# Even mixer of a two-layer trunk: q and k projected first, the convolution's block products inside the attention, the input norm's root on VectorE, the last product by column halves

## The chip, the cores and the metric

The kernel runs on one core of a Trainium2 chip. Its time is the device time of one execution in microseconds (us), and what is compared is the median over runs.

## The reference

A decoder trunk of two layers over 256 tokens of 1024 channels, all in fp32. Each layer is a SwiGLU network (2752 wide), a token mixer and a second SwiGLU network, each on the RMS norm of its input. The mixer of the first layer, the even mixer, is what the change touches:

```
proj = h @ w_in                      # 1024 -> 512 value, 512 gate, 512 q, 128 k, 128 v
u = a_val * sigmoid(a_gate)
u = causal depthwise convolution of u (31 taps, 512 channels) + bias
u = silu(layer_norm(u))
q, k = rms_norm(q), rms_norm(k)      # per head of 64; 8 q heads, 2 kv heads
o = sliding-window attention (window 128, a learned sink per head)
x = x + concat([u, o]) @ w_out
```

## The kernel before

Every weight is fp32 and is multiplied as two parts: `unit` loads half a column block (4 x 128 rows by up to 512 columns) into a `raw` tile, ScalarE rounds it into `hi`, and VectorE writes `lo` = raw - hi. Three raw tiles, four hi and four lo tiles go round. `plan` lists the units in the order of use, `take` hands out the next one and prepares those up to four (`WB`) ahead. A product of 128 tokens with a unit is 12 matmuls: hi with both halves of the input, then lo. The input comes from `Norm`: VectorE applies the gain (`xg`), ScalarE writes the high part of `xt` and VectorE the low part; the square sums go to `rstd_of`, on GpSimd, and the root of the norm (`nr`) is multiplied in after the product.

The even mixer (`even_rest`) has TensorE and VectorE in an order written out by hand; ScalarE's order is a scheduler's. The convolution is shared out: 256 channels run on VectorE, tap after tap (62 steps on tiles `acc`, handed out by `run(taps, n)`), and 256 as 64 block products on TensorE (`pc`, handed out by `run(conv, n)`), each two matmul instructions in the trace. TensorE's share needs its tokens sorted by parity (`PARITY`), and the root of the norm in that order (`parities`, tile `rp`).

Before the change the steps are: projection of value and gate for VectorE's share; of value and gate for TensorE's share (tokens by parity); of q; of k and v; then 20 block products; the norms of q and k; their transposes (`pq`, `pk`); 8 block products; the attention's eight heads, each with scores (`sc`), the softmax's maximum on VectorE and its exponential on ScalarE (`p`), three transposes two heads later (`pp`) and the values (`o`) three heads later, with block products and three taps in between (`fill`); the transposes of the convolution's result (`cn`), its layer norm, transposes back (`yt`), a silu; and the output product in two halves of its inputs, first the attention's half (`mixer_first`, tile `oth`), then the convolution's (`mixer_last`, tile `uth`), each over four banks `m` (two token tiles by two column halves `d`). Then x is updated (`x`), transposed (`pt`) and goes into the next network's first products (`pj`).

Of the kernel before, what the change touches and what calls it, by code (L numbers as in the profile page):

```python
# [16 lines left out]
F32 = mybir.dt.float32  # L17
# [11 lines left out]
S = 256  # L29
# [12 lines left out]
def tile_trunk(ctx: ExitStack, tc: tile.TileContext, x, norm_g, w_gate, w_up, w_down,  # L42
# [18 lines left out]
    def sbank(name):  # L61
        return psum.tile([128, 512], F32, name=name, tag="sc", bufs=2)
# [74 lines left out]

    EV_CUTS = (((512, 256), (0, 256)), ((768, 256), (256, 256)), ((1024, 512),), ((1536, 256),))
    OD_CUTS = (((0, 512),), ((512, 512),), ((1024, 512),), ((1536, 512),))
# [15 lines left out]
    def prepare(n):  # L155
        while len(ready) < min(n, len(plan)):
            run(unit())
# [32 lines left out]

    def take():
        prepare(cursor[0] + WB)
        cursor[0] += 1
        return ready[cursor[0] - 1]
# [84 lines left out]
    class Norm:  # L279
# [15 lines left out]
        def parities(self):  # L295

            ps = tbank("rT")
            for t in range(2):
                nc.tensor.transpose(ps[:, t * 128:t * 128 + 128], self.r[t].to_broadcast([128, 128]), ident)
            rp, junk = sm("rp", 2), nat("junk")  # L300
            for r in range(2):
                nc.vector.tensor_tensor(junk[:, 0:128], ps[:, r:S:2], ident, op=ALU.mult)
                nc.vector.tensor_reduce(rp[:, r:r + 1], junk[:, 0:128], axis=AX.X, op=ALU.add)
            return rp
# [3 lines left out]

    def projects(xp, cols, tokens=HALVES):

        ps = [bank(f"pj{t}") for t in range(2)]

        def steps():
            for kh in range(2):
                hi, lo = take()
                for t in range(2):
                    h, l = (xp.xt[kh][:, i, :, tokens[t]] for i in range(2))
                    yield from products(ps[t], h, l, hi, lo, cols, FULL, kh == 0, kh == 1)
        return ps, steps()
# [72 lines left out]
    def after_(nxt, t, d):  # L392
        if nxt is None:
            nc.sync.dma_start(out=out[0, t * 128:(t + 1) * 128, d * 512:(d + 1) * 512], in_=xs[t][d])
        else:
            nxt.part(t, d)
            if t == 1 and d == 1:
                nxt.finish()

# [72 lines left out]

    def attention_out(os_, ls, fill=lambda t: None):
        rl = work.tile([128, 8, 2], F32, name="rl", tag="rl", bufs=1)
        nc.vector.reciprocal(rl, ls)
        on = []
        for t in range(2):
            on.append(nat("on"))
            nc.vector.tensor_tensor(on[t].rearrange("p (h e) -> p h e", e=64),
                                    os_[t].rearrange("p (h e) -> p h e", e=64),  # L480
                                    rl[:, :, t:t + 1].to_broadcast([128, 8, 64]), op=ALU.mult)
        pts = [transposed(on[t]) for t in range(2)]
        res = []
        for t in range(2):
            fill(t)
            res.append(split_tile(pts[t], "ot"))
        return res
# [3 lines left out]

    def mixer_first(ys, src):

        for d in range(2):
            hi, lo = take()
            for t in range(2):
                yield from products(ys[t][d], *src[t], hi, lo, 512, FULL, True, False)

    def mixer_last(ys, src, nxt):


        units = [take() for d in range(2)]
        n = 4 // len(src[0])
        todo = []
        for j in range(len(src[0])):
            last = j == len(src[0]) - 1
            for d in range(2):
                hi, lo = units[d]
                for t in range(2):
                    h, l = src[t][j]  # L510
                    ks = slice(n * j, n * j + n)
                    product(ys[t][d], h, l, hi[:, ks], lo[:, ks], 512, FULL[:n], False, last)
                    if last:
                        run(todo, len(todo) - 1)
                        nc.vector.tensor_tensor(xs[t][d], ys[t][d], xs[t][d], op=ALU.add)
                        todo.append(partial(after, nxt, t, d))
        return todo
# [17 lines left out]
    def even_rest(xp, nxt, gv):  # L535
# [25 lines left out]
        def pe_conv():  # L561
            pc = sbank("pc")
            for g in range(4):
                for q in range(16):
                    w = wT[4 * g + q // 4][:, 2 * (q % 4):2 * (q % 4) + 2].rearrange("p i c -> p (i c)")
                    yield partial(nc.tensor.matmul, pc[:, g * 128:(g + 1) * 128], w,
                                  vT[g // 2][:, g % 2, q + 1:q + 129], start=q == 0, stop=q == 15)
            for g in range(4):
                yield partial(nc.scalar.activation, cv[:, g], pc[:, g * 128:(g + 1) * 128], AF.Identity,
                              bias=bias2[:, g:g + 1])  # L570

        cv = work.tile([128, 4, 128], F32, name="cv", tag="cv", bufs=1)
        taps = [partial(dve_tap, c, k) for k in range(TAPS) for c in range(2)]
# [8 lines left out]

        rp = xp.parities()
        u = [nat("u") for t in range(2)]
        for t in range(2):
            gated(gv[t], xp.r[t], u[t][:, :256].rearrange("p (g c) -> p g c", c=64))
        gv, steps = projects(xp, 512, PARITY)
        for t in range(2):
# [4 lines left out]
        run(steps, 6)  # L593
        run(taps, 6)
        run(steps)
        run(taps, 8)
        u2 = nat("u2").rearrange("p (g r c) -> p g r c", g=4, r=2)
        for t in range(2):
            gated(gv[t], rp[:, t:t + 1], u2[:, :, t])
        qps, steps = projects(xp, 512)  # L600
        run(steps, 12)
        pt = transposed(u2.rearrange("p g r c -> p (g r c)"))
        for j in range(2):
            nc.scalar.activation(vT[j][:, :, PADB:PADB + 128], pt[:, 2 * j:2 * j + 2], AF.Copy)
        run(steps, 12)
        run(taps, 7)
        run(steps)
        run(taps, 6)
        hs = work.tile([128, 20], F32, name="hs", tag="hs", bufs=1)
        qns = [head_sums(qps[t], xp.r[t], 8, hs[:, 8 * t:8 * t + 8], "q") for t in range(2)]  # L610
        run(taps, 4)
        kps = project(xp, 256)
        run(taps, 3)
        kns = [head_sums(kps[t], xp.r[t], 2, hs[:, 16 + 2 * t:18 + 2 * t], "k") for t in range(2)]
        rh = inv_sqrt(hs, 1.0 / 64, 20)
        run(conv, 20)
        vn = []
        kT = work.tile([128, 512], F32, name="kT0", tag="kT0", bufs=1)
        qT = [slot("qT", "l") for t in range(2)]
        kns = [head_norm(kns[t], rh[:, 16 + 2 * t:18 + 2 * t], 2) for t in range(2)]  # L620
        qns = [head_norm(qns[t], rh[:, 8 * t:8 * t + 8], 8, paired=True) for t in range(2)]
        for t in range(2):
            k_to_T(kns[t], vo[:, 17:18], 1, [kT], t)
        for t in range(2):
            q_to_T(qns[t], gq_e, qT[t])
        for t in range(2):
            v = work.tile([128, 512], F32, name="vn", tag="vn", bufs=2)
            nc.scalar.activation(v[:, :128], kps[t][:, 128:256], AF.Copy, scale=xp.r[t])
            vn.append(v)
        run(conv, 8)  # L630
        run(taps, 4)

        def fill(i):
            run(taps, 3)
            run(conv, 6 if i < 3 else 3)

# [11 lines left out]
        nc.vector.tensor_tensor(ls, ls, es, op=ALU.add)  # L648
        run(taps)
        run(conv)  # L650

        cps = [sbank("cn") for j in range(2)]
# [6 lines left out]
        of = [[cps[0][:, r * 256:(r + 1) * 256], cps[1][:, (1 - r) * 256:(2 - r) * 256]] for r in range(2)]  # L659
        o = attention_out(os_, ls)  # L660
        st, mv = sm("st", 24), sm("mv", 4)
# [4 lines left out]
        r_ = inv_sqrt(mv.rearrange("p (t m) -> p t m", m=2)[:, :, 1], 1.0, 2)  # L666
        ys = mixer_banks()
        steps = mixer_first(ys, o)
        run(steps, 20)
        yn = [nat("yn") for r in range(2)]  # L670
        for j in range(2):
            for r in range(2):
                nc.vector.tensor_scalar(yn[r][:, j * 256:(j + 1) * 256], of[r][j], mv[:, 2 * r:2 * r + 1], r_[:, r:r + 1],
                                        op0=ALU.subtract, op1=ALU.mult)
        us = [[], []]
        for j in range(2):
            run(steps, 6)
            ps = tbank("yt")
# [13 lines left out]
            for t in range(2):  # L692
                us[t].append([w[:, :, HALVES[t]] for w in (hi, lo)])
        run(steps)
        return mixer_last(ys, us, nxt)
# [171 lines left out]
```

## Time and profile before

| | |
|---|---|
| median of three runs | 959.21 us (958.87 to 959.63) |
| the profiled execution's own time | 959.92 us |
| its span in the trace | 957.9 us, 11336 instructions |
| busy share: TensorE matmul, weight load, VectorE, ScalarE, GpSimd | 98%, 81%, 56%, 47%, 10% |
| the even mixer, from its first product to the point from which the next network runs on | 196.67 to 311.56 us |

The time outside the span is 2.0 us. Windows count in us from the span's start. PE is TensorE's matmuls, PEld its weight loads, DVE VectorE, ACT ScalarE, POOL GpSimd. A matmul's end in the trace is modelled, so that two that follow each other overlap in their records; how fast TensorE goes is read from one start to the next.

### The profile page before, as it was taken

The numbers are of one execution on the slowest core, as the hardware profiler recorded it, in microseconds if no ns is written. First come the engines' busy times: TensorE is split into PE (matmuls) and PEld (weight loads), VectorE is DVE, ScalarE is ACT, GpSimd is POOL, SyncE is SP. The second block draws the span as 40 slices with busy tenths as digits, with TensorE's granted clock in tenths as the row PEclk, the third lists the DMA queues.
The fourth block names the chain that finished last, engine by engine and source line by source line (L and its number), as shares of the span: only waits on it lengthen the run. The fifth ranks groups of instructions, "written<-read, shape, count | busy, mean of one in ns | idle before, by whom it ended". The sixth has DMA issues, their size and how long they took to land.

```text
span 957.9 us, 11336 instructions
## 1 busy us (share of the span) xinstructions
PE 936.5 (98%) x4431; PEld 775.5 (81%) x4431; DVE 537.0 (56%) x735; ACT 451.4 (47%) x654; POOL 100.6 (10%) x158
## 2 busy tenths in 40 slices
PE   7999999989898999999999999999999999999998
PEld 5888887868886888888778888887788888888876
DVE  6855464668766655545546554635562275555551
ACT  6644454345444544444445444534567464444430
POOL 3000000740000200000002000000153260000000
PEclk9999999999999999999999999999999999999999
DMA  8865555646204465555665555556653066555540
GB/s 291 274 210 176 176 176 181 194 132 176 89 1 158 150 220 176 155 190 182 197 203 193 176 176 172 180 184 222 213 182 132 3 223 216 184 186 179 187 143 23
DMA packets 91974, 164.75 MB, mean 172 GB/s; under 512 B 3824, under 2 KB 17968, under 8 KB 91920
## 3 DMA queue, kind: packets, MB, share of 16 engines
q1 hardware_dynamic: 91120, 163.07, 52.3%
q0 software_dynamic: 736, 0.93, 0.3%
q8 instruction: 35, 0.57, 0.2%
q14 instruction: 19, 0.16, 0.0%
q10 hardware_dynamic: 64, 0.02, 0.0%
HBM read 162.96 MB, written 1.05 MB: 171 GB/s over the span
## 4 chain that ended last, share of the span: by engine, by line
PE 95%; DVE 3%; ACT 1%; DMA 1%; issue 0%; POOL 0%; DVEq 0%; POOLq 0%
PE pj L333 57%; PE y L199 25%; PE pt L236 3%; PE m L199 2%; PE m L333 2%; DVE lo L330 1%; PE pc L333 1%; PE sc L437 1%; DMA sink_b<-in_ev_sinks_dram 1%; PE pp L451 1%; ACT hi L330 0%; PE sc L438 0%; PE o L459 0%; PE o L458 0%; PE o L457 0%
## 5 line engine op out<-in xcount | busy, mean ns | idle before, releaser
L330 DVE TENSOR_TENSOR lo<-raw,hi 128x1024 fp32r<-128x1024 f32 (+2 forms) x306 | 358.5, 1207 | 237.6 <-ACT hi L330 231.4
L330 ACT ACTIVATE hi<-raw 128x1024 fp32r<-128x1024 f32 (+3 forms) x311 | 308.5, 1039 | 319.3 <-PE pj L333 145.7
L333 PE MATMUL pj<-hi,xt 128*128 128x512 f32 (+2 forms) x1664 | 411.5, 387 | 2.6 <-ACT xt L330 1.9
L333 PEld LDWEIGHTS pj<-hi,xt 128*128 128x128 f32 x1664 | 309.1, 189 | 63.0 <-ACT xt L330 2.6
L333 PE MATMUL pj<-lo,xt 128*128 128x512 f32 (+2 forms) x832 | 224.8, 386 | 0.0
L333 PEld LDWEIGHTS pj<-lo,xt 128*128 128x128 f32 x832 | 154.5, 188 | 28.1
L199 PE MATMUL y<-hi,hth 128*128 128x512 f32 x352 | 138.5, 393 | 0.0
L199 PE MATMUL y<-hi,htl 128*128 128x512 f32 x336 | 131.5, 391 | 0.0
L199 PE MATMUL y<-lo,hth 128*128 128x512 f32 x352 | 100.8, 397 | 0.0
L199 PEld LDWEIGHTS y<-lo,hth 128*128 128x128 f32 x352 | 65.4, 188 | 18.3 <-issue 5.6
L199 PEld LDWEIGHTS y<-hi,hth 128*128 128x128 f32 x352 | 66.1, 188 | 16.0 <-issue 2.9
L199 PEld LDWEIGHTS y<-hi,htl 128*128 128x128 f32 x336 | 63.1, 188 | 12.7
L360 DVE SCALAR_TENSOR_TENSOR h<-pj,nr,sg 128x512 f32<-128x512 f32 (+1 forms) x48 | 33.3, 693 | 38.6 <-PE pj L333 38.5
L330 ACT ACTIVATE hth<-pt 128x512 fp32r<-128x512 f32 x40 | 23.8, 596 | 59.7 <-PE pt L236 59.7
L330 DVE TENSOR_TENSOR htl<-pt,hth 128x512 fp32r<-128x512 f32 x40 | 27.5, 690 | 32.2 <-ACT hth L330 32.2
L353 ACT ACTIVATE sg<-pj,nr 128x512 f32<-128x512 f32 (+1 forms) x48 | 30.3, 634 | 30.3 <-PE pj L333 25.5
L275 POOL TENSOR_TENSOR s<-ss 128x2 f32<-128x2 f32 x5 | 4.0, 794 | 325.3 <-ACT junk L270 325.3
L236 PE MATMUL pt<-ident,h 128*128 128x128 f32 x176 | 27.6, 272 | 0.0
L330 POOL TENSOR_TENSOR lo<-raw,hi 128x2048 fp32r<-128x2048 f32 x5 | 23.4, 4687 | 35.6 <-ACT hi L330 35.6
L236 PEld LDWEIGHTS pt<-ident,h 128*128 128x128 f32 x176 | 22.1, 140 | 5.4
L330 DVE TENSOR_TENSOR xg<-pt,g_n 128x512 f32<-128x512 f32 x24 | 16.5, 687 | 16.8 <-PE pt L236 16.8
L557 DVE SCALAR_TENSOR_TENSOR acc<-uT,cw,acc 128x256 f32<-128x256 f32 x60 | 25.0, 479 | 0.0
(184 smaller groups left out, 547.7 us busy)
## 6 DMA issues: line engine op xcount, KB each, us to landing
raw<-in_ffn_w_up_dram SPq DMA_DIRECT2D x40, 1024.0 KB, 5.2
raw<-in_ffn_w_down_dram SPq DMA_DIRECT2D x40, 1024.0 KB, 5.0
raw<-in_ffn_w_gate_dram SPq DMA_DIRECT2D x38, 1024.0 KB, 5.1
raw<-in_od_w_in_dram SPq DMA_DIRECT2D x8, 1024.0 KB, 5.0
raw<-in_ev_w_in_dram SPq DMA_DIRECT2D x10, 512.0 KB, 4.0
raw<-in_od_w_out_dram SPq DMA_DIRECT2D x4, 1024.0 KB, 5.0
raw<-in_ffn_w_gate_dram SPq DMA_DIRECT2D x8, 384.0 KB, 3.4
raw<-in_ffn_w_up_dram SPq DMA_DIRECT2D x8, 384.0 KB, 4.1
```

Of the source, the lines that this page charges most:

```text
L199: f()
L236: nc.tensor.transpose(ps[:, j * 128:(j + 1) * 128], src[:, j * 128:(j + 1) * 128], ident)
L275: eng.tensor_tensor(s2, sv[:, :, 0], sv[:, :, 1], op=ALU.add)
L330: steps.pop(0)()
L333: f()
L353: nc.scalar.activation(s[:, :n], gs[t], AF.Silu, scale=xp.r[t])
L360: nc.vector.scalar_tensor_tensor(h[:, :n], us[t] if fg == 5 else us[t][:, :], xp.r[t], sg[t][:, :n], op0=ALU.mult, op1=ALU.mult)
L437: nc.tensor.matmul(sc[:, 0:256], qT[1][pr, cq], kk, start=True, stop=True)
L451: nc.tensor.transpose(ps[:, j * 128:(j + 1) * 128], p[i][:, j * 128:(j + 1) * 128], ident)
L557: nc.vector.scalar_tensor_tensor(acc[c], src, w, acc[c], op0=ALU.mult, op1=ALU.add)
```

## The change

The projections are reordered to: value and gate for VectorE's share, q, k and v, then value and gate for TensorE's share. The gating of TensorE's share and its transposes move into the first heads of the attention; its 64 block products now start at the fourth head (six per head) and their last 22 run after the last head's values, around the transposes of the attention's output. They get a bank of the projections' pool, so both score banks serve the scores. Taps per head go from three to five, so that fewer run ahead of the attention. Two units of the output weights are prepared inside the attention (fourth and seventh head). The layer norm's transposes come after four products of the output's first half, and 24 more products come before the transposes back. The second half goes through one column half at a time. The root of the mixer's input norm moves from GpSimd to VectorE, and the parity form of it takes one VectorE operation per parity where it took two.

```diff
-    EV_CUTS = (((512, 256), (0, 256)), ((768, 256), (256, 256)), ((1024, 512),), ((1536, 256),))
+    EV_CUTS = (((512, 256), (0, 256)), ((1024, 512),), ((1536, 256),), ((768, 256), (256, 256)))
...
-                nc.vector.tensor_tensor(junk[:, 0:128], ps[:, r:S:2], ident, op=ALU.mult)
-                nc.vector.tensor_reduce(rp[:, r:r + 1], junk[:, 0:128], axis=AX.X, op=ALU.add)
+                nc.vector.tensor_tensor_reduce(junk[:, 0:128], ps[:, r:S:2], ident, 1.0, 0.0, ALU.mult, ALU.add,
+                                               rp[:, r:r + 1])
...
-                nxt.finish()
+                nxt.finish(nc.vector if nxt.n == 1 else nc.gpsimd)
...
     def mixer_last(ys, src, nxt):
-        units = [take() for d in range(2)]
         n = 4 // len(src[0])
         todo = []
-        for j in range(len(src[0])):
...
+        for d in range(2):
+            hi, lo = take(WB - 1)
+            for t in range(2):
+                for j, (h, l) in enumerate(src[t]):
                     ks = slice(n * j, n * j + n)
+                    product(ys[t][d], h, l, hi[:, ks], lo[:, ks], 512, FULL[:n], False, j == len(src[t]) - 1)
+                run(todo)
+                nc.vector.tensor_tensor(xs[t][d], ys[t][d], xs[t][d], op=ALU.add)
+                todo.append(partial(after, nxt, t, d))
+            prepare(cursor[0] + WB - 1)
         return todo
...
-            pc = sbank("pc")
+            pc.append(bank("pc"))
...
+        qps, steps = projects(xp, 512)
...
+        kps, steps = projects(xp, 256)
+        run(steps, 24)
         qns = [head_sums(qps[t], xp.r[t], 8, hs[:, 8 * t:8 * t + 8], "q") for t in range(2)]
+        run(steps)
+        run(taps, 2)
+        gv, steps = projects(xp, 512, PARITY, WB - 1)
+        run(steps, 8)
...
+        run(steps, 32)
+        run(taps, 6)
         for t in range(2):
             k_to_T(kns[t], vo[:, 17:18], 1, [kT], t)
+        run(steps, 2)
         for t in range(2):
             q_to_T(qns[t], gq_e, qT[t])
+        run(steps)
+        u2 = nat("u2").rearrange("p (g r c) -> p g r c", g=4, r=2)
 
         def fill(i):
-            run(taps, 3)
-            run(conv, 6 if i < 3 else 3)
+            if i == 0:
+                for r in range(2):
+                    gated(gv[r], rp[:, r:r + 1], u2[:, :, r])
+            elif i == 2:
+                pt = transposed(u2.rearrange("p g r c -> p (g r c)"))
+                for j in range(2):
+                    nc.scalar.activation(vT[j][:, :, PADB:PADB + 128], pt[:, 2 * j:2 * j + 2], AF.Copy)
+            elif i > 2:
+                run(conv, 6)
+            run(taps, 5)
+            if i in (3, 6):
+                prepare(cursor[0] + WB - 2 + i // 3)
...
+        o = attention_out(os_, ls, lambda t: run(conv, 4), lambda: run(conv, 8))
         run(conv)
+        for g in range(4):
+            nc.scalar.activation(cv[:, g], pc[0][:, g * 128:(g + 1) * 128], AF.Identity, bias=bias2[:, g:g + 1])
+        ys = mixer_banks()
+        steps = mixer_first(ys, o, WB - 1)
+        run(steps, 4)
```

On TensorE, where the second half of the inputs of the first projection is awaited, before the change (`pj_1584` and `pj_1585` are this projection's two token tiles):

```order
L236 MATMUL pt<-ident,x_83 128x128 x4
L333 MATMUL pj_1585<-lo,xt 128x512
L333 MATMUL pj_1584<-hi,xt 128x512
L333 MATMUL pj_1585<-hi,xt 128x512
L333 MATMUL pj_1584<-hi,xt 128x512 x7
L333 MATMUL pj_1584<-lo,xt 128x512 x4
```

The same place of the changed kernel, where these tiles are `pj_1580` and `pj_1581`, and `pj_1699` is q's projection of the first token tile:

```order
L237 MATMUL pt<-ident,x_83 128x128 x4
L334 MATMUL pj_1581<-lo,xt 128x512
L334 MATMUL pj_1699<-hi,xt 128x512 x8
L334 MATMUL pj_1699<-lo,xt 128x512
L334 MATMUL pj_1580<-hi,xt 128x512
L334 MATMUL pj_1581<-hi,xt 128x512
L334 MATMUL pj_1580<-hi,xt 128x512 x7
```

Nine products of q's first half stand ahead of the products that need the second half of the input.

On ScalarE, ahead of the first head, in the changed kernel (`pj_1874` and `pj_1875` are the projection for TensorE's share of the convolution, `sg` its gates):

```order
L576 ACTIVATE sg<-pj_1874,rp 128x256
L525 ACTIVATE kT_1914<-pk,vo 128x128 x2
L519 ACTIVATE qT<-pq,gq_e 128x512 x2
L331 ACTIVATE hi<-raw 128x1024 x2
L576 ACTIVATE sg<-pj_1875,rp 128x256
L446 ACT_TABLE_LOAD
L446 ACTIVATE p,ls<-p,nm 128x256
L446 ACTIVATE p,ls<-p,nm 128x128
```

Before the change the table load followed straight on the two `qT`; now a unit's rounding and the second gate stand between them.

On VectorE, from the first head's maximum to the second's, in the changed kernel (`u_1998` is the gated value of TensorE's share):

```order
L443 ISA p,nm<-sc,m_even,sink_n 128x256
L443 ISA nm 128x1
L443 ISA p,nm<-sc,m_even,sink_n 128x128
L443 ISA nm 128x1
L578 SCALAR_TENSOR_TENSOR u_1998<-pj_1874,rp,sg 128x4x64
L578 SCALAR_TENSOR_TENSOR u_1998<-pj_1875,rp,sg 128x4x64
L556 SCALAR_TENSOR_TENSOR acc_1688<-uT,cw,acc_1688 128x256
L556 SCALAR_TENSOR_TENSOR acc_1689<-uT,cw,acc_1689 128x256
L556 SCALAR_TENSOR_TENSOR acc_1688<-uT,cw,acc_1688 128x256
L556 SCALAR_TENSOR_TENSOR acc_1689<-uT,cw,acc_1689 128x256
L556 SCALAR_TENSOR_TENSOR acc_1688<-uT,cw,acc_1688 128x256
L443 ISA p,nm<-sc,m_even,sink_n 128x256
```

Before the change three taps stood between two heads and no gating; behind the fourth and the seventh head the two halves of a unit's `lo` now follow the five taps.

## Rows read from the trace of the kernel before

**Rows 1.** The page's table of busy time.

```profile
PE 936.5 (98%) x4431; PEld 775.5 (81%) x4431; DVE 537.0 (56%) x735; ACT 451.4 (47%) x654; POOL 100.6 (10%) x158
```

**Rows 2.** Busy time by window: stretch, its length, PE, PEld, DVE, ACT, POOL, clock, DMA.

```profile
196.67:311.56 114.89, 103.87 (x582) 88.06 (x581) 81.34 (x190) 54.91 (x114) 6.37 (x17) 0.97 0.36 109
```

**Rows 3.** Waits of TensorE from 196 to 315: total us, times, longest.

```profile
PE pk L236 <- DVE k L414: 2.8, 1, 2.8
...
PE pj L333 <- ACT xt L330: 1.9, 2, 1.3
...
PE pj L333 <- DVE xt L330: 0.5, 1, 0.5
```

**Rows 4.** The chain that ended last, in order of time: start, us, what.

```profile
62.70 20.00 PE pj L333 x88
...
226.79 0.44 PE pt L236 x4
```

**Rows 5.** Windows of slow clock and of waits.

```profile
249.30:252.60 3.30, 3.28 (x16) 3.30 (x17) 2.12 (x6) 2.08 (x4) 0.00 (x0) 0.50 0.03 6
253.70:275.00 21.30, 21.30 (x154) 19.03 (x153) 15.71 (x57) 10.27 (x39) 0.00 (x0) 1.00 0.00 1
...
280.00:283.40 3.40, 3.40 (x14) 2.61 (x13) 1.88 (x4) 1.20 (x2) 0.00 (x0) 0.51 0.00 0
288.80:290.40 1.60, 0.16 (x1) 0.00 (x0) 1.60 (x3) 0.84 (x1) 0.00 (x0) 1.00 0.00 0
306.30:308.70 2.40, 0.04 (x1) 0.00 (x0) 2.40 (x4) 0.32 (x2) 0.00 (x0) 1.00 0.00 0
```

**Rows 6.** Timeline: ScalarE in the projections (start, us, engine, line, operation).

```profile
202.00 2.00 ACT L330 ACTIVATE hi<-raw 128x1024 fp32r<-128x1024 f32 x2 [3.26 <-issue]
...
217.61 1.15 ACT L330 ACTIVATE hi<-raw 128x512 fp32r<-128x512 f32 x2
...
221.35 0.48 ACT L579 ACTIVATE sg<-pj,rp 128x256 f32<-128x256 f32 x1 [2.58 <-issue]
```

**Rows 7.** Timeline: taps, block products and the norms of q and k.

```profile
237.76 1.67 DVE L557 SCALAR_TENSOR_TENSOR acc<-uT,cw,acc 128x256 f32<-128x256 f32 x4
...
241.01 4.63 PE L333 MATMUL pc<-vT,wT 128*128 128x128 f32 x40
...
245.58 0.18 DVE L243 TENSOR_SCALAR nv<-hs 128x20 f32<-128x20 f32 x1
...
248.41 1.43 DVE L420 TENSOR_TENSOR qn<-q,nr 128x256 f32<-128x256 f32 x4
```

**Rows 8.** Timeline: the attention's heads and the second table load.

```profile
253.68 0.70 PE L437 MATMUL sc<-kT,qT 64*128 64x256 f32 x2
...
254.64 0.48 DVE L442 CUSTOM_DVE_ANT_0 p<-sc,m_even,sink_n 128x256 f32<-128x256 f32 x1 [3.21 <-PE sc L438]
...
255.32 1.27 DVE L557 SCALAR_TENSOR_TENSOR acc<-uT,cw,acc 128x256 f32<-128x256 f32 x3
...
261.11 0.70 PE L437 MATMUL sc<-kT,qT 64*128 64x256 f32 x2
...
263.78 0.70 PE L437 MATMUL sc<-kT,qT 64*128 64x256 f32 x2
...
275.48 1.28 ACT L338 ACT_TABLE_LOAD   x1
```

**Rows 9.** Timeline: from the last heads to the layer norm.

```profile
276.73 0.39 PE L459 MATMUL o<-vn,pT 128*128 128x64 f32 x2
...
283.46 0.75 DVE L664 BATCH_NORM_STATS2 st<-cn 128x6 f32<-128x256 f32 x2
283.81 0.39 PE L333 MATMUL m<-hi,oth 128*128 128x512 f32 x1
...
287.48 2.36 DVE L330 TENSOR_TENSOR lo<-raw,hi 128x1024 fp32r<-128x1024 f32 x2
...
289.75 1.89 DVE L673 TENSOR_SCALAR yn<-cn,mv,nr 128x256 f32<-128x256 f32 x4
```

More of the change, by code (lines that the diff above doesn't have):

```diff
@@ L189, in unit, with take @@
         return steps
-    def take():
-        prepare(cursor[0] + WB)
+    def take(ahead=WB):
+        prepare(cursor[0] + ahead)
         cursor[0] += 1
@@ L307, in tile_trunk, with projects @@
     PARITY = [slice(r, S, 2) for r in range(2)]
-    def projects(xp, cols, tokens=HALVES):
+    def projects(xp, cols, tokens=HALVES, ahead=WB):
         ps = [bank(f"pj{t}") for t in range(2)]
@@ L314, in steps @@
             for kh in range(2):
-                hi, lo = take()
+                hi, lo = take(ahead)
                 for t in range(2):
@@ L471, in attention, with attention_out @@
         return os_, nm, ls
-    def attention_out(os_, ls, fill=lambda t: None):
+    def attention_out(os_, ls, fill=lambda t: None, first=lambda: None):
         rl = work.tile([128, 8, 2], F32, name="rl", tag="rl", bufs=1)
@@ L481, in attention_out @@
                                     rl[:, :, t:t + 1].to_broadcast([128, 8, 64]), op=ALU.mult)
+        first()
         pts = [transposed(on[t]) for t in range(2)]
@@ L490, in mixer_banks, with mixer_first @@
         return [[bank(f"m{t}{d}") for d in range(2)] for t in range(2)]
-    def mixer_first(ys, src):
+    def mixer_first(ys, src, ahead=WB):
         for d in range(2):
-            hi, lo = take()
+            hi, lo = take(ahead)
             for t in range(2):
@@ L499, in mixer_last @@
     def mixer_last(ys, src, nxt):
-        units = [take() for d in range(2)]
         n = 4 // len(src[0])
         todo = []
-        for j in range(len(src[0])):
[L506 to L510, printed above, removed]
-                    ks = slice(n * j, n * j + n)
[L512 to L516, printed above, removed]
+        for d in range(2):
+            hi, lo = take(WB - 1)
+            for t in range(2):
+                for j, (h, l) in enumerate(src[t]):
+                    ks = slice(n * j, n * j + n)
+                    product(ys[t][d], h, l, hi[:, ks], lo[:, ks], 512, FULL[:n], False, j == len(src[t]) - 1)
[3 more added lines that the diff above has]
+            prepare(cursor[0] + WB - 1)
         return todo
@@ L565, in pe_conv @@
                     w = wT[4 * g + q // 4][:, 2 * (q % 4):2 * (q % 4) + 2].rearrange("p i c -> p (i c)")
-                    yield partial(nc.tensor.matmul, pc[:, g * 128:(g + 1) * 128], w,
+                    yield partial(nc.tensor.matmul, pc[0][:, g * 128:(g + 1) * 128], w,
                                   vT[g // 2][:, g % 2, q + 1:q + 129], start=q == 0, stop=q == 15)
-            for g in range(4):
-                yield partial(nc.scalar.activation, cv[:, g], pc[:, g * 128:(g + 1) * 128], AF.Identity,
-                              bias=bias2[:, g:g + 1])
+        pc = []
         cv = work.tile([128, 4, 128], F32, name="cv", tag="cv", bufs=1)
@@ L581, in gated @@
             nc.vector.scalar_tensor_tensor(dst, v[0], r, v[1], op0=ALU.mult, op1=ALU.mult)
-        rp = xp.parities()
         u = [nat("u") for t in range(2)]
@@ L586, in even_rest @@
             gated(gv[t], xp.r[t], u[t][:, :256].rearrange("p (g c) -> p g c", c=64))
-        gv, steps = projects(xp, 512, PARITY)
+        qps, steps = projects(xp, 512)
         for t in range(2):
@@ L593, in even_rest @@
         run(steps, 6)
[L594 to L606, printed above, removed]
+        rp = xp.parities()
+        run(taps, 4)
         run(steps)
@@ L609, in even_rest @@
         hs = work.tile([128, 20], F32, name="hs", tag="hs", bufs=1)
+        kps, steps = projects(xp, 256)
+        run(steps, 24)
         qns = [head_sums(qps[t], xp.r[t], 8, hs[:, 8 * t:8 * t + 8], "q") for t in range(2)]
-        run(taps, 4)
-        kps = project(xp, 256)
-        run(taps, 3)
+        run(steps)
+        run(taps, 2)
+        gv, steps = projects(xp, 512, PARITY, WB - 1)
+        run(steps, 8)
         kns = [head_sums(kps[t], xp.r[t], 2, hs[:, 16 + 2 * t:18 + 2 * t], "k") for t in range(2)]
+        vn = []
+        for t in range(2):
+            v = work.tile([128, 512], F32, name="vn", tag="vn", bufs=2)
+            nc.scalar.activation(v[:, :128], kps[t][:, 128:256], AF.Copy, scale=xp.r[t])
+            vn.append(v)
         rh = inv_sqrt(hs, 1.0 / 64, 20)
-        run(conv, 20)
-        vn = []
         kT = work.tile([128, 512], F32, name="kT0", tag="kT0", bufs=1)
@@ L621, in even_rest @@
         qns = [head_norm(qns[t], rh[:, 8 * t:8 * t + 8], 8, paired=True) for t in range(2)]
+        run(steps, 32)
+        run(taps, 6)
         for t in range(2):
             k_to_T(kns[t], vo[:, 17:18], 1, [kT], t)
+        run(steps, 2)
         for t in range(2):
             q_to_T(qns[t], gq_e, qT[t])
[L626 to L631, printed above, removed]
-        def fill(i):
-            run(taps, 3)
-            run(conv, 6 if i < 3 else 3)
+        run(steps)
+        u2 = nat("u2").rearrange("p (g r c) -> p g r c", g=4, r=2)
+        def fill(i):
+            if i == 0:
[10 more added lines that the diff above has]
+                prepare(cursor[0] + WB - 2 + i // 3)
         es = work.tile([128, 8, 2], F32, name="es", tag="es", bufs=1)
@@ L659, in even_rest @@
         of = [[cps[0][:, r * 256:(r + 1) * 256], cps[1][:, (1 - r) * 256:(2 - r) * 256]] for r in range(2)]
-        o = attention_out(os_, ls)
         st, mv = sm("st", 24), sm("mv", 4)
@@ L666, in even_rest @@
         r_ = inv_sqrt(mv.rearrange("p (t m) -> p t m", m=2)[:, :, 1], 1.0, 2)
-        ys = mixer_banks()
-        steps = mixer_first(ys, o)
-        run(steps, 20)
         yn = [nat("yn") for r in range(2)]
@@ L674, in even_rest @@
                                         op0=ALU.subtract, op1=ALU.mult)
+        run(steps, 24)
         us = [[], []]
         for j in range(2):
-            run(steps, 6)
             ps = tbank("yt")
@@ L693, in even_rest @@
                 us[t].append([w[:, :, HALVES[t]] for w in (hi, lo)])
+            run(steps, 6)
+        prepare(ev0 + 13)
         run(steps)
```

## The prediction

> **What bounds the kernel now.** I read the table of busy time first: TensorE's matmuls are busy for 936.5 of 957.9 us, VectorE for 56%, ScalarE for 47% [rows 1]. So time comes only from places where TensorE stands still or runs slowly, and the change touches one stretch of it, the even mixer. From its first product to the point from which the next network runs on are 114.89 us, in which TensorE's records fill 103.87 [rows 2]. By these two numbers 11.0 us are to be had there.
>
> The list of waits names the largest: 2.8 for k, 1.9 and 0.5 for the mixer's input [rows 3]. But a wait's record is not all of a loss, and so I went from one start to the next. The paces at full clock: 88 products in 20.00, 0.227 each; four transposes in 0.44, 0.11 each [rows 4]; 40 block-product instructions in 4.63, 0.116 each, two to a block product [rows 7]. What five places cost beyond that:
>
> - a, the second half of the input: 1.9 + 0.5 = 2.4 [rows 3].
> - b, from the end of the 40 instructions, 245.64, to the first scores, 253.68 [rows 7, 8]: 8.0 for 10 transposes (1.1) and 16 instructions (1.9). Lost 5.0: the wait of 2.8, and the clock, at 0.50 for 3.3 us [rows 5].
> - c, from the last but one head's values, 277.12, to the fifth output product, 283.81 [rows 9]: 6.7 for three value products (some 0.6, an estimate from the 0.39 of their last two records), 16 transposes (1.8) and four products (0.9). Lost 3.4; the clock is at 0.51 in half of it [rows 5].
> - d, the layer norm's result: 1.6 with 0.16 busy [rows 5]. Lost 1.4.
> - e, x and the next input: 2.4 with 0.04 busy [rows 5]. Lost 2.4.
>
> Together 14.6. The Trainium skill, "Perfetto Trace Analysis", section "Identifying the Most-Contended Engine", says that matmul busy time is a poor measure of the room left, because matmuls are pipelined. By the busy records the sum below would be 11.0 less the 4.5 of new waits, 6.5; by starts it is larger. The trace agrees with the page: c and b hold losses that the busy column counts as work.
>
> **The change part by part.** Products, transposes and block products stay the same in number; only their places move, so each place is costed by what it then waits for.
>
> *Place a.* Nine products of q (2.0) now stand ahead of the wait, and the rounding of a unit that stands before the input's on ScalarE has 256 columns, not 512: 1.15 in place of 2.00 [rows 6]. 2.0 + 0.85 is more than 2.4: loss 0; without the shorter rounding it would be 0.4. The root of the norm on VectorE has some 13 short steps; twelve such steps with k's scaling take 2.8 from 245.58 to 248.41 [rows 7]. They lie behind 22 products (5.0) that come before the gated values are transposed: 0, at worst 2.8. The one-step form of the parity root is not in the trace; the nearest row, the attention's maximum, takes 0.48 for twice the columns [rows 8]. It is two operations of a VectorE that has slack there: 0, at worst 1.0.
>
> *Place b.* Root, k and q take 2.8 + 1.43 [rows 7], the sums some 0.5 (an estimate), and now lie behind 40 products, 9.1 us, of the last projection; with two taps and a unit's two `lo` halves (2.36 [rows 9]) ahead on VectorE that is some 8: loss 0, at worst the old 2.8. No block product stands there.
>
> *The attention.* Count from the first scores' start. Before, the maximum starts 0.96 behind the scores and takes 0.68 with its reads (254.64 to 255.32) [rows 8]; a tap costs 0.40 (four in 1.67, three in 1.27) [rows 7, 8]. TensorE does scores one to three in 2.7. ScalarE meanwhile finishes a unit's rounding, which begins about 0.5 before the first scores (it waits for the last product with the tile that it overwrites): 2.00, then the second gate 0.48, then the table load 1.28 [rows 6, 8], then the first exponential, some 0.5. The first probabilities are there at 3.8: **TensorE waits 1.1**. VectorE gates behind the same ScalarE row until 2.4, five taps to 4.4, second maximum to 5.1. TensorE has done three transposes and four by 4.6 and needs a score bank that this maximum frees: **0.5**, and **0.2** for the second exponential.
>
> From there VectorE does 0.68 + 5 x 0.40 = 2.68 per head and twice 2.36 for `lo`: the eighth maximum ends at 5.1 + 6 x 2.68 + 4.7 = 25.9, its exponential at 26.7. TensorE's head with six instructions took 2.67 (261.11 to 263.78) [rows 8]; with twelve it takes 2.67 + 0.70 = 3.37, so that five heads from 5.1 on, and one without scores (2.5), end at 24.6. It waits **2.1** for the eighth head, with 28 ready block products queued behind it. Sum 3.9. VectorE sets this stretch's length: every us that it gets later here is a us at the end, and the early waits cost nothing of their own beyond that.
>
> *Place c.* Behind the last values now stand 28 instructions (3.2), which cover the scaling of the output on VectorE, then its transposes, then 16 instructions (1.9), which cover rounding and `lo` of it (some 0.6 each, estimates from 512 columns of [rows 6, 9]); four output products stand ahead of the layer norm's transposes and cover the copy of the block products. Loss of waits 0, at worst the old 1.3.
>
> *Place d.* The norm's statistics and root take 4.0 (283.46 to 287.48), a scaling 0.47 (four in 1.89) [rows 9]: 4.5, behind 24 products (5.4) in place of the 20 after which they started late. The unit's 2.36 that stood in between is done in the attention. Loss 0, at worst 1.4.
>
> *Place e.* The first column half is ready 24 products before the second, so the next network's first products can fill in. But add, transposes, gain, high and low part (some 0.65 each) lie behind 12 products (2.7) at each token tile, which is close: 0.6, between 0 and 1.2.
>
> *The clock.* It fell twice, once behind the 2.8 of place b and once in place c, where transposes and short value products surround a wait [rows 5]; in the attention with block products it held 1.00 from 253.70 to 275.00 [rows 5]. In the changed kernel the first three heads have no block products and waits of 1.8, and the eighth has a wait of 2.1. A fall early is hidden by VectorE; one behind the eighth head is not. A stretch of 3.3 at 0.50 costs at most 1.7. I take 1.1, between 0 and 3.4.
>
> Sum after: 3.9 + 0.6 + 1.1 = 5.6. Gain 14.6 - 5.6 = 9.0. The profiled execution took 959.92 (957.9 of span and 2.0 around it), which gives 950.9; the median shown is 0.71 lower: **950 us**. Beyond the mixer the networks run on as before; a unit more or less that is prepared ahead is no bound there, since the DMA stands at 0.00 in the attention [rows 5].
>
> **The rivals.**
> 1. *The gain half eaten by VectorE or ScalarE.* The attention hangs on hand-made order: 35 taps and two `lo` units pass VectorE between the first maximum and the eighth, and a tap of 0.48 in place of 0.40 (a mean of 0.42, as 1.67 / 4 has it, would add 0.7) adds 2.8; a later table load or rounding adds its 1 to 2 in full. For it: nothing covers VectorE there. Against it: three and four taps in a row show 0.40. It gives 952.7 to 957.
> 2. *Slower: the clock stays low through the attention.* Place: from the projections' end until block products come thick again. TensorE's work from first scores to the eighth head is 22.8 at full clock; in place b, 3.3 us at half clock did about two thirds to a half of the work. If all of it ran so, it would take 34 to 46 in place of 26.7, and the gain is gone from 9 us of it on: 961 to 969. It decides when the clock is low for more than some 25 of these us. For it: the fall in place c with the same kinds of instructions. Against it: 1.00 for 21 us with half as many block products per head.
> 3. *The time freed is taken back behind the mixer*, because the next network's units, its bank or its norm's root are late when TensorE comes 9 us earlier: no change, 957.3 to 961. For it: that root stays on GpSimd. Against it: products of the network's up half can go first.
> 4. *More than forecast*: clock, place e and two of the attention's waits cost nothing: below 945.
>
> **How the numbers follow.** Forecast (945 to 952.7) 0.60, rival 1 0.22, rival 2 0.07, rival 3 0.08, rival 4 0.03. The range is 945 to 957: its ends are a gain of 14 (the bounds of zero) and of 2.2 (rival 1). Within 0.2%, 1.9 us, a measurement of this kernel can't well tell it from no change. Faster: 0.60 + 0.22 + 0.03, less 0.02 for rival 1's end, 0.83; same 0.09, rival 3 with that 0.02 and without 0.01 that ends beyond it; slower 0.08, rival 2 with that 0.01.
>
> **What would show it.** The stretch from the mixer's first product to the first undisturbed one of the network should take 105 to 107 in place of 114.9. TensorE's waits for k and for the layer norm's result should be gone, those for the input and x below 1; new ones for the first and the eighth head's probabilities, 1.1 and 2.1, with 26 us on VectorE without a pause but the one behind the second gate. Wrong would be: a wait for q, k or the layer norm as long as before; the eighth head's wait above 4; the clock at 0.50 for more than two stretches; a new wait in the network that follows.

## The result and the profile after

The changed kernel takes 954.97 us (median of 6 runs, 953.23 to 956.97), the kernel before 959.61 in the same job: a ratio of 0.9943, interval 0.992 to 0.9966. The gain is 4.6, half of the 9.0 forecast. The profiled execution took 955.37, its span is 953.3.

What answers to [rows 1], the page's table of busy time after:

```profile
PE 938.3 (98%) x4431; PEld 777.9 (82%) x4431; DVE 537.9 (56%) x748; ACT 451.2 (47%) x654; POOL 98.9 (10%) x142
```

TensorE's records grew by 1.8 while the time fell: a sign that the column can't say where time went. TensorE's waits after, from 190 to 340, which answer to [rows 3]:

```profile
PE pj L334 <- ACT sg L354: 3.1, 1, 3.1
PE pp L452 <- ACT p L446: 1.1, 1, 1.1
PE sc L438 <- DVE nm L443: 0.8, 1, 0.8
PE pj L334 <- DVE xt L331: 0.2, 1, 0.2
PE pj L334 <- ACT xt L331: 0.2, 1, 0.2
```

The waits for k, for the mixer's input, for the layer norm and for x are gone. The early ones of the attention (1.1 and 0.8) were forecast, the eighth head's (2.1) did not come, and one of 3.1 stands first that no term had: in the next network, for the gate's activation.

For the account I cut the span at four starts on TensorE: the last down product of the first network, the first scores, the last values, the first output product, and the next network's first down product. The four windows of before, then of after (columns as in [rows 2]):

```profile
196.24:253.68 57.44, 51.80 (x278) 43.94 (x278) 44.40 (x91) 29.00 (x49) 6.80 (x18) 0.97 0.52 153
253.68:279.05 25.37, 24.05 (x177) 21.64 (x177) 16.13 (x59) 13.63 (x47) 0.00 (x0) 1.00 0.00 1
279.05:282.02 2.97, 2.97 (x19) 2.71 (x19) 1.31 (x3) 0.60 (x1) 0.00 (x0) 0.65 0.00 0
282.02:434.32 152.30, 148.24 (x689) 123.08 (x689) 89.62 (x111) 70.87 (x91) 6.21 (x16) 1.00 0.53 170
```

```profile
194.82:237.20 42.38, 42.38 (x219) 35.32 (x218) 34.44 (x80) 24.93 (x44) 2.31 (x2) 1.00 0.60 165
237.20:269.84 32.64, 30.73 (x193) 27.89 (x192) 28.94 (x86) 16.54 (x49) 0.00 (x0) 0.79 0.28 93
269.84:275.71 5.87, 5.87 (x56) 5.87 (x55) 2.53 (x4) 1.08 (x2) 0.00 (x0) 1.00 0.00 0
275.71:429.69 153.98, 150.38 (x700) 124.78 (x699) 86.35 (x108) 71.11 (x94) 9.28 (x16) 0.99 0.49 161
...
241.00:254.50 13.50, 13.50 (x56) 12.03 (x57) 13.50 (x40) 6.12 (x23) 0.00 (x0) 0.51 0.10 22
```

Read the lengths: projections 57.44 to 42.38, attention 25.37 to 32.64 (it now holds the block products), the output's start 2.97 to 5.87, and the rest, which should have become some 2 us shorter, went from 152.30 to 153.98. The sum fell by 3.2. The last row shows the granted clock at 0.51, TensorE's lower level of 1.2 GHz, for 13.5 us of the attention, where I allowed for a cost of 1.1. From the end of this sum to the end of TensorE's last record are 519.9 to 520.0 in every profile of this study. What lies ahead of it varies: the first network's last down product starts between 194.0 and 197.8, with nothing changed there, and of the 4.6 between these two profiled spans 1.4 stems from that. So the experiments below are compared by these four lengths beside their times.

### The profile page after: what moved, and what is told of

Same layout as the page of the kernel before. It is cut to its first block, busy times and chain, and to the rows that moved or that the text cites. A ratio compares the mean times of both kernels' runs of the same rounds, so it can differ in the third digit from the quotient of the medians.

```text
span 953.3 us, 11336 instructions
## 1 busy us (share of the span) xinstructions
PE 938.3 (98%) x4431; PEld 777.9 (82%) x4431; DVE 537.9 (56%) x748; ACT 451.2 (47%) x654; POOL 98.9 (10%) x142
## 4 chain that ended last, share of the span: by engine, by line
PE 84%; issue 12%; POOL 2%; DMA 1%; ACT 0%; DVE 0%; POOLq 0%
PE pj L334 53%; PE y L200 24%; PE pt L237 3%; PE m L334 1%; PE m L200 1%; POOL wT L547 1%; DMA sink_b<-in_ev_sinks_dram 1%; PE sc L438 0%; PE pp L452 0%; POOL na L250 0%; PE o L460 0%; PE o L459 0%; PE pp L738 0%; PE p L743 0%; PE sc L439 0%
```

## The experiments

All lengths in one table: projections, attention, output's start, rest, and their sum, each from one profiled execution; then the ratio to the kernel before with its interval, from all executions. The attention's length depends on a low clock whose duration changes from one execution to the next (see again), so sums are compared with that in mind.

| kernel | proj. | att. | start | rest | sum | ratio |
|---|---|---|---|---|---|---|
| before | 57.44 | 25.37 | 2.97 | 152.30 | 238.08 | |
| changed | 42.38 | 32.64 | 5.87 | 153.98 | 234.87 | 0.9943 (0.992 to 0.9966) |
| again | 42.34 | 29.92 | 5.87 | 154.15 | 232.28 | 0.9927 (0.9903 to 0.9952) |
| root2 | 42.35 | 29.97 | 5.87 | 153.29 | 231.48 | 0.9913 (0.9885 to 0.994) |
| dense | 42.37 | 29.63 | 5.87 | 154.05 | 231.92 | 0.9929 (0.9904 to 0.9953) |
| hold | 41.94 | 33.34 | 8.55 | 154.07 | 237.90 | 1.0001 (0.9989 to 1.0014) |
| late | 42.34 | 29.60 | 5.87 | 152.99 | 230.80 | 0.9927 (0.9899 to 0.9955) |
| late_dense | 42.33 | 29.63 | 5.87 | 153.63 | 231.46 | 0.9926 (0.9899 to 0.9952) |
| light | 42.34 | 29.63 | 5.87 | 152.55 | 230.39 | single run |
| oldlast | 42.34 | 30.05 | 5.87 | 150.57 | 228.83 | 0.9905 (0.9877 to 0.9934) |
| oldlast2 | 42.33 | 30.16 | 5.87 | 150.54 | 228.90 | 0.9893 (0.9874 to 0.9912) |
| early_x | 42.34 | 32.68 | 5.87 | 150.85 | 231.74 | 0.9899 (0.9881 to 0.9917) |
| before_halves | 57.48 | 25.37 | 2.91 | 155.76 | 241.52 | 1.0038 (1.0022 to 1.0053) |
| oldlast_dense | 42.34 | 29.62 | 5.87 | 151.70 | 229.53 | 0.9899 (0.9877 to 0.9922) |

**again**, the changed kernel unaltered.

> The changed kernel once more, for comparison on the same chip. If the losses read in its trace are of the kernel and not of one execution, TensorE's clock is again at half for 10 to 14 us within the attention, the first up products of the next network again wait some 3 us behind the root on GpSimd, and the time is 954 to 956. If they were chance, the low stretch is 7 us or less, or the wait below 1.

953.63. The wait for the root is there as before, 3.1, so it belongs to the kernel. The clock was low for a shorter time: the first stretch of it is half as long (the trace's clock steps give 6.8 us, 13.7 in the first profile), and the attention took 29.92 in place of 32.64. What decides between the two lengths no run settles. Of the profiles with these heads, five show 6.8 us and an attention of 29.6 to 30.2 (again, root2, late, oldlast, oldlast2), and two show 13.7 us and 32.6 to 32.7 (the first one and early_x). Here is the place of the wait in this profile: TensorE, then VectorE, ScalarE and GpSimd (start, length, engine, line, operation).

```profile
316.66 1.07 PE L334 MATMUL pj<-lo,xt 128*128 128x512 f32 x4
320.80 3.25 PE L334 MATMUL pj<-hi,xt 128*128 128x512 f32 x8 [3.07 <-ACT sg L354]
...
307.94 0.68 DVE L513 TENSOR_TENSOR x<-m,x 128x512 f32<-128x512 f32 x1
308.54 6.89 DVE L331 TENSOR_TENSOR lo<-raw,hi 128x1024 fp32r<-128x1024 f32 x6
315.35 0.68 DVE L331 TENSOR_TENSOR xg<-pt,g_n 128x512 f32<-128x512 f32 x1
317.29 2.39 DVE L331 TENSOR_TENSOR lo<-raw,hi 128x1024 fp32r<-128x1024 f32 x2 [1.25 <-ACT hi L331]
...
316.19 2.01 ACT L331 ACTIVATE hi<-raw 128x1024 fp32r<-128x1024 f32 x2 [6.75 <-DMA raw<-in_ffn_w_gate_dram]
320.06 0.69 ACT L354 ACTIVATE sg<-pj,nr 128x512 f32<-128x512 f32 x1 [1.86 <-POOL nr L255]
320.64 0.62 ACT L331 ACTIVATE xt<-xg 128x512 fp32r<-128x512 f32 x1
...
309.52 0.29 POOL L276 TENSOR_TENSOR s<-ss 128x2 f32<-128x2 f32 x1 [111.33 <-ACT junk L271]
...
311.02 1.05 POOL L245 TENSOR_SCALAR ny<-nv 128x2 int32<-128x2 int32 x1
312.16 1.08 POOL L246 TENSOR_SCALAR nv<-nv 128x2 f32<-128x2 f32 x1
...
316.42 0.20 POOL L250 TENSOR_TENSOR na<-na,nv 128x2 f32<-128x2 f32 x1
...
317.54 1.05 POOL L250 TENSOR_TENSOR na<-na,nv 128x2 f32<-128x2 f32 x1
...
319.83 0.19 POOL L255 TENSOR_TENSOR nr<-nr,na 128x2 f32<-128x2 f32 x1
```

VectorE does six low parts of three units, 6.89, right behind its last sum for x and ahead of the last piece of the input (`xg`). The root's chain on GpSimd starts at 309.52 and ends at 320.02. Its steps take 1.0 to 1.1 while VectorE writes low parts (308.54 to 315.43, 317.29 to 319.68), all but the first one (0.29), and 0.2 between them. The gate's activation (`sg`) waits for the root, its bank with it, and TensorE for the bank. The same row delays the input too: `xg` is done at 316.03, but on ScalarE a unit's rounding and then the gate stand ahead of its high part, which starts at 320.64.

**root2** moves that root to VectorE.

```diff
-                nxt.finish(nc.vector if nxt.n == 1 else nc.gpsimd)
+                nxt.finish(nc.vector if nxt.n in (1, 2) else nc.gpsimd)
```

> The root of the norm behind the even mixer on VectorE too. Theory: GpSimd's chain of 10 us, whose steps take 1.05 where they took 0.2 to 0.5 elsewhere, is the cause of the 3.1 us wait and of the half clock behind it; both go, and the time falls by 3 to 4.5, to 950.5 to 952. Rival: VectorE is just as late there, as its units' low parts take 7 us in the same stretch; the root waits behind them, the wait stays at 2 to 3, and the time is 954 to 956.

952.44, the rest 0.9 shorter. The wait that ended with the gate is gone, but TensorE now waits for pieces of the input, 2.7 in place of 0.5:

```profile
PE pj L334 <- ACT xt L331: 1.5, 2, 1.1
PE pj L334 <- DVE xt L331: 1.2, 2, 0.9
```

The root itself came no sooner. Its last step on VectorE, and then the last input piece and the gates on ScalarE:

```profile
323.88 0.16 DVE L252 SCALAR_TENSOR_TENSOR nr<-na,nr 128x2 f32<-128x2 f32 x1
...
320.05 0.61 ACT L331 ACTIVATE xt<-xg 128x512 fp32r<-128x512 f32 x1
326.86 1.25 ACT L354 ACTIVATE sg<-pj,nr 128x512 f32<-128x512 f32 x2
```

The root is done at 324.04, 48.2 behind the first output product, where again had 46.0. What changed is ScalarE's order: the input's last piece no longer stands behind the gate, and TensorE has products to do while the root is late. Nor did the half clock go: it stands at 0.50 for 3.4 us from 323.4. So GpSimd's slow chain alone is not the loss: the last piece of the input is about as late as the root, and until one of the two is there TensorE has nothing to do.

**dense** adds 18 block products to the first three heads (they write columns of a bank that later values overwrite).

```diff
+            if pad is not None and i < 3:
+                for _ in range(6):
+                    nc.tensor.matmul(os_[0][:, 384:512], *pad, start=True, stop=True)
             fill(i)
...
```

> Six block products of 128 columns more in each of the first three heads (18, whose results are overwritten; 4.2 us of TensorE at full clock, as the kernel before had them there). Clock theory: the clock stays at full through the attention, the heads are again set by VectorE, and the stretch from first scores to last values falls from 32.5 to about 29.5, the time to 951 to 953 in spite of 4.2 us more work. Rival (VectorE sets the attention in any case and the low clock is hidden): the stretch stays at 32 to 33 and the time at 954.5 to 956. Second rival (TensorE's work sets it): the time rises by up to 4.2, to 959.

953.42. The clock stays at full through the attention, all of TensorE's waits there go, and 4.2 us of work more cost nothing:

```profile
237.23:266.86 29.63, 29.63 (x229) 27.31 (x228) 28.82 (x86) 16.43 (x49) 0.00 (x0) 1.00 0.30 102
```

29.63 here, 29.92 with 6.8 us of low clock, 32.64 with 13.7: the long low stretch costs 2.7 more than the short one. What the short one costs is not shown, since no run has full clock without the 18 products.

**light** leaves out, from dense, 30 of the taps that VectorE does in the heads.

```diff
-            run(taps, 5)
+            run(taps, {0: 5, 7: 5, 8: 4}.get(i, 0)) if i < 9 else taps.clear()
```

> The 18 block products more, and 30 of the taps, those that VectorE does between the second and the eighth head, left out (the output of that half of the convolution lacks them). Theory (VectorE sets the attention, as forecast): from first scores to last values falls from 29.6 to 27.5 to 28.3, TensorE's own rate. Rival (TensorE or ScalarE sets it): 29.3 to 29.9.

950.01 in a single run. The attention is the same to the hundredth, though VectorE's busy time in it fell from 28.82 to 17.52:

```profile
236.34:265.97 29.63, 29.63 (x229) 27.31 (x228) 17.52 (x56) 16.22 (x49) 0.00 (x0) 1.00 0.31 104
```

So with the 18 products TensorE sets this stretch. It says less of the changed kernel: by my count TensorE's eighth turn stood at 24.6 and VectorE's at 26.7; 24.6 with 4.2 more and the early waits (1.8) less is 27.0, beyond VectorE. (The turns are counted from the first scores.) The run also has the 3.3 wait for the root, but no half clock behind it, and its rest is 1.5 shorter than that of dense: from one run, an estimate of what that half clock costs.

**hold** puts two products of the last projection into each of the first three heads.

```diff
-        run(steps)
...
+            run(steps, 2)
-            if i == 0:
+            if i == 2:
...
-            elif i == 2:
+            elif i == 4:
...
-            elif i > 2:
+            elif i > 4:
                 run(conv, 6)
```

> The last six products of the last projection are held back, two in each of the first three heads, with the second gate, its transposes and the block products two heads later. Clock theory: denser first heads shorten the low stretch; with 1.4 us of products moved into TensorE's free time the time falls by 1.4 to 4.5, to 950.5 to 953.5. Rival (two products a head, 0.45 us, are too few for the clock, and later block products bring heads without any): the clock stays low as long or longer, and the time is 954 to 957.

960.02: the whole gain gone, and worse than its rival said. The low clock stayed at 13.7 us, TensorE waited 3.2 for probabilities, in two heads, and 12 block products more were left behind the last values, 2.7 of the output's start (8.55 in place of 5.87).

**late** leaves the units behind the last product to the next network.

```diff
-            prepare(cursor[0] + WB - 1)
+            prepare(cursor[0] + (0 if d else WB - 1))
         return todo
```

> The preparing of units that stands behind the mixer's last product is left to the next network's own takes, so that VectorE no longer has three units' six low parts (6.9 us) ahead of the last piece of the input, beside which GpSimd's root steps took 1.05 each. Theory (these low parts are the loss behind the mixer): the wait for the root of 3.1 and the half clock behind it go, the stretch from the mixer's first output product to the next network's first down product falls from 154.0 to 149.5 to 150.5, and the time by 3.5 to 4.5 against the changed kernel's 953.6, to 949 to 950.5. Rival (the units are then late themselves, as the input piece was): waits for units of 2 to 4 take their place, and the time is 952.5 to 956.

953.05. The root's chain now takes 4.5, every step some 0.2, with VectorE idle beside it, and TensorE's wait for it is gone. Two of its rows, and then the waits for the input's pieces that stand in its place:

```profile
314.71 0.19 POOL L244 TENSOR_SCALAR nv<-s 128x2 f32<-128x2 f32 x1 [0.25 <-POOL s L276]
...
318.55 0.20 POOL L255 TENSOR_TENSOR nr<-nr,na 128x2 f32<-128x2 f32 x1
```

```profile
PE pj L334 <- ACT xt L331: 2.9, 2, 2.2
...
PE pj L334 <- DVE xt L331: 1.0, 1, 1.0
```

The rest is 1.2 shorter, not 4. The theory that the low parts slow the root holds; that the place of these six is the whole loss falls: the units are now prepared ahead of other pieces of the input, on the same two engines.

**late_dense** has late's edit and dense's.

> The later units together with the 18 block products more in the first three heads, which hold the clock at full. If both losses are separate they add up: the attention takes 29.6 from first scores to last values, and the stretch behind the mixer 149.5 to 150.5; 948.5 to 950. If the low clock in the first heads is hidden by VectorE, as the equal times of dense and of the changed kernel have it, it is the same as with the later units alone, within 0.5.

953.32, as late alone within what can be told.

**oldlast** and **oldlast2** are the changed kernel with the last product in the order of before: both column halves of the first chunks, then the last chunk of each half and token tile.

```diff
-        for d in range(2):
-            hi, lo = take(WB - 1)
-            for t in range(2):
-                for j, (h, l) in enumerate(src[t]):
...
+        units = [take() for d in range(2)]
+        for j in range(len(src[0])):
+            last = j == len(src[0]) - 1
+            for d in range(2):
+                hi, lo = units[d]
+                for t in range(2):
+                    h, l = src[t][j]
...
```

> The mixer's last product in the order of the kernel before, all else as changed. By the forecast of place e alone, this costs 1.8: 955.4. By the theory of the later units the column halves brought the wait of 3.1 and the half clock with them, and undoing them gives back about 4 and costs 1.8: 951 to 952, with no wait for the root.

> The mixer's last product in the order of the kernel before, all else as changed, once more. If the column halves cost what its first run showed (the stretch from the first network's last product to the second's first down product 228.8, against 232.3 with them), that stretch is again within 0.5 of 228.8 and the time 951 to 952.5, a ratio of 0.990 to 0.992. If that was one execution's chance, 231 to 233 and 953 to 955.

951.78 and, with more runs on another chip, 950.69. The rest falls from 154.1 to 150.6 and 150.5. The times alone say less: the intervals of their ratios overlap that of again. TensorE's waits in the second:

```profile
PE pt L237 <- DVE x L517: 2.4, 1, 2.4
PE sc L438 <- DVE nm L443: 1.1, 2, 0.8
PE pp L452 <- ACT p L446: 1.1, 1, 1.1
```

The old wait of 2.4 for x is back, the one for the root gone, and no half clock follows. The root is late here too (321.2), but no input piece is:

```profile
297.39 2.36 DVE L331 TENSOR_TENSOR lo<-raw,hi 128x1024 fp32r<-128x1024 f32 x2 [4.97 <-ACT hi L331]
299.67 1.28 DVE L517 TENSOR_TENSOR x<-m,x 128x512 f32<-128x512 f32 x2
...
315.10 0.68 DVE L331 TENSOR_TENSOR xt<-xg,xt 128x512 fp32r<-128x512 f32 x1
```

The last piece of the input is written at 315.78, 40.3 behind the first output product (275.52); in again it is written at 321.98, 48.0 behind it (274.00). With the whole input there, TensorE has products for its other banks while the root is late, as in root2.

**before_halves** is the kernel before with the column halves alone: oldlast's diff the other way round.

> The kernel before with the last product by column halves alone. By the forecast of place e it gains 1.8: a ratio of 0.998. By the theory of the low parts (three units' pieces on VectorE ahead of the input's last piece, root beside them) it costs 1.5 to 3.5: a ratio of 1.0015 to 1.0035, with a wait for the root or for the input's pieces behind the mixer. If the wait needs the changed attention, which prepares units in other places, it gains as forecast.

963.42, slower by 3.8 than the kernel before in the same series (959.63), the rest 3.5 longer. The same wait comes with them:

```profile
PE pj L333 <- ACT sg L353: 3.1, 1, 3.1
...
PE pj L333 <- ACT xt L330: 2.1, 3, 1.3
```

So the edit that brings the halves costs 3.5, in the kernel before as in the changed one (3.6). It holds two things, the order of the products and the places at which units are prepared. Late moves the last preparing alone and gives back 1.2; no run has the order of the halves with the units prepared as before, so how the 3.5 divides between the two is open.

**early_x** prepares one unit fewer ahead of oldlast's sums for x, and **oldlast_dense** adds dense's products to it.

```diff
-        units = [take() for d in range(2)]
+        units = [take(WB - d) for d in range(2)]
```

> The last product in the order of before, with one unit fewer prepared ahead of it, so that VectorE's two sums for x no longer stand behind that unit's low parts (2.36), which wait for its rounding. Theory: the wait of 2.4 for x goes and nothing else comes, the stretch falls from 228.8 to 226.5 to 227.5, the time to 949 to 950.5. Rival (the unit put off is late itself in the next network, as with the later units): waits of 1 to 3 for it or for the input's pieces, and the time is 951 to 953.

> The last product in the order of before and the 18 block products more in the first three heads. The clock stays at full in the attention, which takes 29.6 from first scores to last values. If a low clock there costs nothing but what it takes from VectorE's slack, up to 6.8 us of it at least, the time is that of the kernel without the 18, 950.5 to 951.5. If the low stretch, 6.8 us in some executions and 13.7 in others, costs 2 to 3 us in part of them, the time is 949 to 950.5, and its runs lie closer together.

950.57 and 950.89, not to be told from oldlast2. In early_x the wait for x went, and 2.7 for the input's pieces came, as its rival had it; its profile caught the long low clock, which is why its attention and its sum are longer than oldlast2's. In oldlast_dense the attention held its clock and the wait for x was followed by a half clock (rest 1.2 longer). The version to keep is the changed kernel without the column halves, 0.989 to 0.991 of before.

## Why the prediction was half right

The time lies in the range, and the direction and most of the mechanism held; half of the gain went into one step that I priced with the wrong sign. That the range took this in is luck: its upper part stood there for rival 1, VectorE as the limit of the attention, which no run shows. By its steps:

- **Places a and b.** Forecast: 7.4 of loss gone, 60 short instructions and transposes (6.9) moved away, 57.44 to 43.1. Measured 42.3, no wait and the clock at 1.00. Right.
- **The attention.** The early waits are 1.1 and 0.8 to 1.1, forecast 1.8. The eighth head's turn was forecast 26.7 behind the first scores; it starts at 27.1 in again and at 29.8 in the first profile, with no wait. The 26.8 of dense and light is near the forecast by chance, as TensorE sets it there. One sum in the working is off: five heads of 3.37 and one of 2.5 from 5.1 on end at 24.45, not 24.6, which makes the forecast wait 2.2 to 2.3.
- **The clock**, forecast 1.1 (0 to 3.4). I held that an early fall is hidden by VectorE and charged one behind the eighth head. It fell early, 3.4 to 5.2 us behind the first scores, and the long stretch was not hidden: it cost 2.7 more than the short one. With some 1.5 (the estimate from light) behind the new wait, which had no term, the first profile is beyond the bound. Rival 2's mechanism was there for up to 13.7 us, short of the 25 from which I had it decide.
- **Places c and d.** Forecast 0, measured 0; c's stretch runs at a clock of 1.00.
- **Place e.** This step failed. I counted 0.6 of waits for the input in place of 2.4; the waits are 0.4 to 0.5, but behind them come the 3.1 for the root and its half clock. The rest should have been 152.30 less 1.4 (d) and 2.4 (e), with 0.6 and the layer norm's eight transposes (0.9) added: 150.0. It is 154.0 to 154.2. The step as I put it was "Beyond the mixer the networks run on as before", and a unit more or less prepared ahead no bound "since the DMA stands at 0.00". The bound was not the DMA but VectorE, which writes the units' low parts just where the last pieces of x and of the input are due, and behind it ScalarE's order: in again the last transposes of x end at 311.35, `xg` starts 4.0 later, and the high part 4.6 after `xg` is done. The prediction named "a new wait in the network that follows" as a sign of being wrong, and it came.
- **The rivals.** The time fell into the band of rival 1, but not by its mechanism: no run shows VectorE as the limit of the attention. Rival 3 named the root on GpSimd as late, and against it I set that the up half's products can go first. They do, and last until 317.7 in again; the root came at 320.0. So rival 3's mechanism was there, at about half of its price.

Without the column halves the sum is 228.9, 9.2 below that of before. That this is near the forecast of 9.0 is chance too: without the 1.8 of place e the forecast is 7.2, so the other terms gave some 2 more than they were priced at.

## What to carry to other kernels

When a change lets a stretch end earlier, list what each helper engine does in the 20 us behind it, in its order, before counting that stretch's waits as won: here a forecast gain of 1.8 us on TensorE brought 6.9 us of VectorE's work ahead of the last piece that the next stage needed. An edit of several parts should be priced and timed part by part: one part, alone in the kernel before, was slower by 3.8 us and hid behind the gain of the rest. And when repairs (here root2, late and early_x) each move a wait without a gain in time that can be told, look at the order that made it.

## What the runs showed of the hardware

Small GpSimd steps of 2 columns take 0.2 alone and 1.0 to 1.1 beside VectorE's `lo`, whose pieces take 1.15 each (six in 6.89) and read two operands from SBUF. The 16 steps took 10.5 in again and 4.5 in late. The Trainium skill, "SBUF — State Buffer", section "Who interferes with whom", says that a VectorE instruction with two SBUF inputs contends with a GpSimd instruction that reads SBUF, and that the ports which the two engines share are an exclusive lock. The trace agrees: beside the `lo` pieces one step takes about as long as one piece.

Idle time of TensorE is not all that a wait costs, nor always: behind waits of 3.1 the clock stood at half for 3.4 us in five profiles, and behind the 3.3 of light it did not. Behind the wait of 2.4 for x it did so in oldlast_dense, and not in before, oldlast and oldlast2.
